# Three pairs of gate tiles computed as block products behind the branch-a outputs, with block products summed in PSUM

## The chip, the cores and the metric

The kernel runs on one core of one Trainium2 chip. The metric is the device time of one execution in microseconds (us); three runs of the kernel before gave 1294.07, 1295.1 and 1296.71, a median of 1295.1. The engines are TensorE (PE in the profile; its weight loads are PEld), VectorE (DVE), ScalarE (ACT), GpSimd (POOL) and SyncE (SP), each of which takes its instructions in the order in which they are issued.

## The reference

One step of a hybrid encoder layer on 576 rows (512 of a new stream, 64 of a running one), model width 1024. A half-step SwiGLU FFN of width 2816, a mixer with two convolution branches and gates, a second half-step FFN, a final RMSNorm. What matters here is the mixer:

```python
p = h @ w_in
a_b, a_c, a_v, b_u, gate_a, gate_b = jnp.split(p, cuts, axis=-1)
a_conv, new_a = causal_depthwise_conv(a_c * a_v, hist_a, conv_a_w)
y_a = (a_b * a_conv) @ w_a_out
glu = b_u[..., :D_B] * jax.nn.sigmoid(b_u[..., D_B:])
b_conv, new_b = causal_depthwise_conv(glu, hist_b, conv_b_w)
b_act = jax.nn.silu(layer_norm(b_conv + conv_b_bias, conv_b_ln_g, conv_b_ln_b))
y_b = b_act @ w_b_out
merged = jax.nn.sigmoid(gate_a) * y_a + jax.nn.sigmoid(gate_b) * y_b
x = x + merged @ w_out
```

`gate_a` is called p5 below, `gate_b` p6; each has eight output tiles of 128 columns.

## The kernel before

Activations lie transposed, 128 channels by T = 576 rows per tile, in two halves of H = 288. Every operand of a product is split into a high part and a low part (`high`, `low`), and a tile product is the sum of three: high by high, high by low, low by high. An output tile of a 1024-deep product is 8 deep tiles x 3 x 2 halves = 48 matmuls of 128x128 by 128x288; two of them, a "plain pair", are 96. Most of the FFN's gate and up tiles, and two pairs of the branch-b outputs, are computed as "block pairs" instead: of two output tiles and two halves, seven products of 12 matmuls each (`block`, L452; 84 in all) are taken, on sums and differences of weight tiles (made by `Stream.add`, planned in `plan_block`, L350) and of input halves (`Forms`, L643), and put together from the seven by half-size sums.

In the block pairs of before each of the seven products gets a PSUM bank of its own. ScalarE copies the first bank out (288 columns), and seven half-size sums on VectorE make the two output tiles (`steps` in `pair`, L863, and in `block_pair`, L1240). PSUM is a pool `mm` of four tiles of two banks.

All engine calls go through `Ordered` (L88 in the profile for every instruction), which keeps each engine's instructions in the order of the code. Work that can float is kept in the list `work`; `fill` takes a piece from it whenever an estimate of VectorE's time lags behind an estimate of TensorE's. What has to be done with a finished product is run one product later, by `take`. Weights come through `Stream`: SyncE loads a raw tile, ScalarE casts it to the high part, and the low part is made either by GpSimd's accumulating DMA (`"dma"`; ScalarE then writes the negated high part first) or by VectorE (`"dve"`), some units ahead of their use.

The stage of the change begins when branch a's convolution is done. The loop at L1171 to L1178 alternates p5_j and ya_j, eight of each: `ga_of` has ScalarE take the sigmoid of p5_j out of PSUM, `ya_of` has VectorE multiply ya_j, still in PSUM, by it into `M[j]` (the buffers of x). Beside these products the LayerNorm of branch b goes on, driven by `advance` (L1149): when all eight convolution tiles `C[j]` are there, `lnsum.gather` and a total by a product with ones give the mean; `center` (L1112) subtracts it from a tile on VectorE, has ScalarE square the tile and VectorE add the square; `var.gather` splits the sum into a high part (ScalarE) and a low part (VectorE), a second total by ones gives the variance and `rstd` the factor RL. Then come the eight p6 tiles (`gb_of`, sigmoids on ScalarE) with `swish` of branch b as floating work, the branch-b outputs yb (pairs 0 and 2 plain, 1 and 3 as blocks), and the o product.

The seven products of a pair in before:

```python
for n, xs in enumerate(bs):
    q.append(block(ws.get(plan[f, "s", i][n]), xs))
    if n > 0:
        steps[n - 1]()
```

## Time and profile before

| what | us |
|---|---|
| median of 3 runs | 1295.1 |
| span of the profiled execution | 1290.1 |
| TensorE busy | 1279.4 (99%), 9728 matmuls |
| VectorE busy | 925.1 (72%) |
| ScalarE busy | 765.5 (59%) |
| GpSimd busy | 361.6 (28%) |
| p5 and ya products in the span | 645.0 to 746.2 |
| totals by ones in that stretch | 688.67 (mean), 714.48 (variance) |
| p6 products | 746.2 to 796.1 |
| branch-b outputs | 796.1 to 843.3 |
| second FFN begins | about 901 |

The profile is that of one execution; the time of a run lies about 5 us over the span. In a row of a timeline the first two numbers are start and length in us; the end of a matmul is modelled, so rows of TensorE overlap by a little, and the pace is read from start to start. In brackets stands the idle time ahead of a row and what ended it. A row of groups ends in the count, the busy time, the mean of one in ns and the idle time ahead. A row of stretches has the busy time of PE, PEld, DVE, ACT and POOL, then the granted TensorE clock, the share of DMA and GB/s.

### The profile page before, as it was taken

The page shows a single profiled execution, that of the slowest core. Times are in us where ns is not written, and L with a number is a line of the kernel's source. Part 1 is how long each engine was busy: PE and PEld are TensorE (multiplying, and loading weights), DVE is VectorE, ACT ScalarE, POOL GpSimd, SP SyncE. Part 2 cuts the span into 40 slices and gives each one's busy share as a digit, 9 for nine tenths or more (in the row PEclk, how much of TensorE's full clock was granted, in tenths as well). Part 3 has the DMA queues.
Part 4 walks back from the last instruction along what each step waited for, and adds up shares of the span by engine and source line. Part 5 has one row for each costly group of instructions (what it writes and reads, how often), then busy time and mean ns, then how long its engine had stood idle before and what let it go on. Part 6 is the DMA issues. An engine that isn't in the chain of part 4 may idle for free.

```text
span 1290.1 us, 25702 instructions
## 1 busy us (share of the span) xinstructions
PE 1279.4 (99%) x9728; PEld 1277.5 (99%) x9728; DVE 925.1 (72%) x1539; ACT 765.5 (59%) x1359; POOL 361.6 (28%) x460
## 2 busy tenths in 40 slices
PE   9999999999999999999999999999999999999997
PEld 9999999999999999999999999999999999999997
DVE  6868668748846998888895166656867848847956
ACT  7655646646776645555444576477665655654664
POOL 0032332232333444333321221122142141241230
PEclk9999999999999999999999999999999999999998
DMA  7286787886799898788885767696687696796783
GB/s 220 70 181 154 163 180 155 177 181 149 154 224 232 174 200 173 165 172 174 172 172 124 163 142 154 151 236 145 139 175 171 151 197 151 164 204 138 158 172 97
DMA packets 286812, 215.26 MB, mean 167 GB/s; under 512 B 15456, under 2 KB 248928, under 8 KB 286688
## 3 DMA queue, kind: packets, MB, share of 16 engines
q0 software_dynamic: 56160, 92.43, 43.3%
q1 hardware_dynamic: 228784, 120.35, 32.8%
q8 instruction: 77, 1.26, 0.4%
q10 hardware_dynamic: 1744, 0.83, 0.2%
q14 instruction: 47, 0.39, 0.1%
HBM read 116.17 MB, written 4.98 MB: 94 GB/s over the span
## 4 chain that ended last, share of the span: by engine, by line
PE 92%; issue 4%; DVE 2%; DMA 1%; ACT 1%; POOL 0%; DVEq 0%; POOLq 0%; ACTq 0%
PE mm L88 92%; DVE tmp L88 0%; DMA g<-raw 0%; DMA raw<-in_w_b_out_dram 0%; DVE x L88 0%; DVE g L88 0%; DMA u<-raw 0%; ACT act L88 0%; DVE w L88 0%; POOL u L88 0%; DVE act L88 0%; ACT u L88 0%; ACT w L88 0%; ACT g L88 0%; POOL g L88 0%
## 5 line engine op out<-in xcount | busy, mean ns | idle before, releaser
L88 PE MATMUL mm<-act,u 128*128 128x288 f32 x4758 | 668.3, 293 | 0.1
L88 PEld LDWEIGHTS mm<-act,u 128*128 128x128 f32 x4758 | 638.9, 188 | 0.4 <-DMA u<-raw 0.3
L88 PE MATMUL mm<-act,g 128*128 128x288 f32 x3030 | 432.9, 294 | 0.9 <-DMA g<-raw 0.9
L88 PEld LDWEIGHTS mm<-act,g 128*128 128x128 f32 x3030 | 410.3, 188 | 1.1 <-DMA g<-raw 1.1
L88 POOL DMA_DIRECT2D u<-raw x197 | 172.3, 874 | 481.7 <-ACT u L88 317.4
L88 PE MATMUL mm<-act,act 128*128 128x288 f32 (+2 forms) x1896 | 259.9, 293 | 0.0
L88 PEld LDWEIGHTS mm<-act,act 128*128 128x128 f32 x1896 | 252.2, 188 | 0.5 <-ACT act L88 0.3
L88 ACT CAST u<-raw 128x512 fp32r<-128x512 f32 (+2 forms) x207 | 118.8, 574 | 172.0 <-PE mm L88 136.7
L88 POOL DMA_DIRECT2D g<-raw x126 | 109.9, 872 | 297.4 <-ACT g L88 242.7
L88 DVE SCALAR_TENSOR_TENSOR w<-g,prm,w 128x606 f32<-128x606 f32 x232 | 179.3, 844 | 1.4 <-ACT w L88 1.4
L88 DVE TENSOR_TENSOR tmp<-mm,tmp 128x288 f32<-128x288 f32 (+1 forms) x251 | 112.9, 459 | 70.3 <-PE mm L88 53.7
L88 ACT ACTIVATE u<-u 128x512 fp32r<-128x512 f32 (+2 forms) x197 | 116.8, 593 | 6.2
L88 ACT CAST g<-raw 128x512 fp32r<-128x512 f32 (+2 forms) x136 | 75.1, 553 | 43.9 <-DMA raw<-in_ffn_w_down_dram 17.6
L88 DVE SCALAR_TENSOR_TENSOR tmp<-mm,r 128x576 f32<-128x576 f32 x48 | 36.3, 757 | 76.6 <-PE mm L88 76.6
L88 POOL DMA_DIRECT2D act<-raw x67 | 59.1, 883 | 108.3 <-ACT act L88 94.5
L88 ACT CAST act<-tmp 128x576 fp32r<-128x576 f32 x92 | 61.9, 675 | 43.1 <-DVE tmp L88 42.1
L88 ACT CAST g<-w 128x512 fp32r<-128x512 f32 x79 | 49.0, 620 | 64.4 <-DVE w L88 58.6
L88 ACT CAST u<-w 128x512 fp32r<-128x512 f32 x81 | 50.2, 619 | 61.0 <-DVE w L88 43.6
L88 DVE TENSOR_TENSOR act<-tmp,act 128x576 fp32r<-128x576 f32 x92 | 67.5, 754 | 18.1 <-ACT act L88 16.5
L88 ACT ACTIVATE g<-g 128x512 fp32r<-128x512 f32 (+2 forms) x126 | 72.1, 572 | 4.0
L88 DVE TENSOR_TENSOR w<-raw,raw 128x512 f32<-128x512 f32 x82 | 56.2, 685 | 16.2 <-DMA raw<-in_ffn_w_gate_up_dram 11.2
L88 ACT ACTIVATE tmp<-tmp 128x576 f32<-128x576 f32 x47 | 32.2, 686 | 45.1 <-DVE tmp L88 45.0
(86 smaller groups left out, 830.6 us busy)
## 6 DMA issues: line engine op xcount, KB each, us to landing
raw<-in_ffn_w_gate_up_dram SPq DMA_DIRECT2D x171, 256.0 KB, 3.5
u<-raw POOLq DMA_DIRECT2D x140, 256.0 KB, 4.2
raw<-in_w_in_dram SPq DMA_DIRECT2D x112, 256.0 KB, 3.8
raw<-in_ffn_w_down_dram SPq DMA_DIRECT2D x96, 192.0 KB, 3.8
g<-raw POOLq DMA_DIRECT2D x69, 256.0 KB, 4.2
act<-raw POOLq DMA_DIRECT2D x61, 256.0 KB, 4.4
g<-raw POOLq DMA_DIRECT2D x43, 192.0 KB, 4.5
u<-raw POOLq DMA_DIRECT2D x41, 192.0 KB, 4.5
```

The source lines that it names most:

```text
L88: return self.tc.keep_in_program_order(fn(*args, **kwargs))
```

## The change

Three things change. First, every block pair (39 in the FFNs, two in yb) now goes through one function, `seven`. The order of the second and third product is swapped; products five and six aren't given banks of their own but are summed into the banks of products one and two. ScalarE copies both banks out after product two (576 columns, one instruction), and one finished bank after product six (288 columns); VectorE makes five half-size sums, not seven.

Second, the eight p5 tiles no longer alternate with ya. The order is p5_0, ya_0 to ya_7, p5_1, p6_0, then three block pairs for p5_2 to p5_7, then p6_1 to p6_7. As ya_j now comes ahead of its gate, ScalarE copies it to `M[j]` (for j of 1 to 7), and VectorE multiplies by the gate later (`gated`). The input forms for the blocks are made by VectorE, as sums of the high and low parts that are there, with differences of halves (`whole`) and a split in high and low (`part`).

Third, the mean's total comes between ya_7 and p5_1, and the centring, squares and the variance's total run beside the three block pairs, one step of `between` after each of the 21 products.

```diff
-                (s2, "dve", ((s2, (s1, a11)),)),
-                (s1, "dve", ()),
+                (s1, "dve", ((s2, (s1, a11)),)),
+                (s2, "dve", ()),
...
+    def seven(ws7, xs7, c1, c2, gate, between=None):
+        qq, uu = ttile(), ttile()
+        u2, u3 = half(uu, 0), half(uu, 1)
+        first, second = psum2(), psum2()
+        q = [first[:, 0, :H], first[:, 1, :H], second[:, 0, :H], second[:, 1, :H]]
+        def middle():
+            dve.tensor_tensor(u2, q[2], half(qq, 0), op=ALU.subtract)
+            dve.tensor_tensor(u3, q[3], u2, op=ALU.add)
+            dve.tensor_tensor(half(c2, 1), u3, half(qq, 1), op=ALU.subtract)
+        def close():
+            sca.copy(half(c1, 0), q[0])
+            dve.tensor_tensor(half(c1, 1), q[1], u2, op=ALU.subtract)
+            gate()
+        steps = {
+            1: lambda: sca.copy(halves(qq), first[:, :, :H]),
+            3: middle,
+            5: close,
+        }
+        last = bank()[:, :H]
+        for n, (w, xs) in enumerate(zip(ws7, xs7)):
+            block(ws.get(w), xs, (q + q[:2] + [last])[n], n not in (4, 5))
+            if n in steps:
+                steps[n]()
+            if between:
+                between()
+        return lambda: dve.tensor_tensor(half(c2, 0), last, u3, op=ALU.add)
...
+        def first():
+            sca.activation(c1, c1, AF.Sigmoid)
+            gated(j, c1)
+        def second():
+            final()
+            sca.activation(c2, c2, AF.Sigmoid)
+        def between():
+            take()
+            if later:
+                later.pop(0)()
+            advance()
+            fill()
+        final = seven(plan["p5", "s", i], bs, c1, c2, first, between)
+        later.extend((second, lambda: gated(j + 1, c2)))
```

ScalarE's queue before, from the sigmoid of p5_5 (`tmp_1351`) to that of p5_6 (`tmp_1363`); the rest makes weight parts:

```order
L88 ACTIVATE tmp_1351_9127<-mm_1336_8991 128x576
L88 CAST act_1353_9130<-raw_1332_8933 128x512
L88 ACTIVATE act_1354_9131<-act_1353_9130 128x512
L88 CAST u_1356_9161<-raw_1334_8963 128x512
L88 ACTIVATE u_1356_9161<-u_1356_9161 128x512
L88 CAST u_1359_9193<-raw_1339_8997 128x512
L88 ACTIVATE u_1359_9193<-u_1359_9193 128x512
L88 CAST u_1361_9223<-raw_1341_9027 128x512
L88 ACTIVATE u_1361_9223<-u_1361_9223 128x512
L88 ACTIVATE tmp_1363_9253<-mm_1352_9129 128x576
```

And now, from the close of pair one to the copy of pair two's first two banks (`tmp_1337` is c1 of pair one and `tmp_1338` its c2, `g_969` a tile of the LayerNorm, `mm_1373` the two first banks of pair two):

```order
L88 COPY tmp_1337_9040<-mm_1341_9044 128x288
L88 ACTIVATE tmp_1337_9040<-tmp_1337_9040 128x576
L88 CAST act_1366_9183<-w_1364_9161 128x512
L88 ACTIVATE tmp_1368_9199<-g_969_5725 128x576
L88 CAST u_1376_9211<-raw_1288_8753 128x512
L88 ACTIVATE u_1376_9211<-u_1376_9211 128x512
L88 ACTIVATE tmp_1338_9041<-tmp_1338_9041 128x576
L88 CAST act_1381_9237<-raw_1360_9125 128x512
L88 ACTIVATE act_1382_9238<-act_1381_9237 128x512
L88 COPY tmp_1371_9204<-mm_1373_9206 128x576
```

The sigmoids of pair one, a square of the LayerNorm and four weight instructions stand between the close of pair one and that copy. VectorE's queue, at the last centrings before (`g_1033` and `g_1047` are tiles of the LayerNorm, `tmp_1304` the mean, `x4` a gated output):

```order
L88 TENSOR_TENSOR g_1033_6212<-g_1033_6212,tmp_1304_8758 128x576
L88 TENSOR_TENSOR acc_1306_8765<-acc_1306_8765,tmp_1325_8916 128x576
L88 TENSOR_TENSOR g_1047_6359<-g_1047_6359,tmp_1304_8758 128x576
L88 TENSOR_TENSOR acc_1306_8765<-acc_1306_8765,tmp_1326_8920 128x576
L88 TENSOR_TENSOR tmp_1328_8923<-acc_1306_8765,tmp_1327_8922 128x576
L88 TENSOR_TENSOR x4_94<-mm_1329_8927,tmp_1335_8989 128x576
```

And now, from the middle of pair one to the sum that makes its last half, the one that writes `tmp_1338` from `mm_1343`:

```order
L88 TENSOR_TENSOR tmp_1338_9041<-tmp_1340_9043,tmp_1339_9042 128x288
L88 TENSOR_TENSOR u_1361_9127<-w_1353_9080,u_1361_9127 128x512
L88 TENSOR_TENSOR act_1363_9146<-w_1359_9123,act_1362_9145 128x512
L88 TENSOR_TENSOR w_1364_9161<-w_1353_9080,raw_1347_9055 128x512
L88 TENSOR_TENSOR tmp_1337_9040<-mm_1341_9044,tmp_1340_9043 128x288
L88 TENSOR_TENSOR x2_92<-x2_92,tmp_1337_9040 128x576
L88 TENSOR_TENSOR g_969_5725<-g_969_5725,mu_1351_9075 128x576
L88 TENSOR_TENSOR acc_1352_9077<-acc_1352_9077,tmp_1368_9199 128x576
L88 TENSOR_TENSOR act_1367_9184<-w_1364_9161,act_1366_9183 128x512
L88 TENSOR_TENSOR w_1375_9209<-raw_1348_9057,raw_1349_9059 128x512
L88 TENSOR_TENSOR tmp_1338_9041<-mm_1343_9046,tmp_1340_9043 128x288
```

The centrings now stand among the weight sums and the half-size sums of the pairs. TensorE's queue at the variance's total, before, between two plain products:

```order
L88 MATMUL mm_1344_9056<-tmp_1327_8922,ones_r_83 128x288
L88 MATMUL mm_1344_9056<-tmp_1328_8923,ones_r_83 128x288
L88 MATMUL mm_1344_9056<-tmp_1327_8922,ones_r_83 128x288
L88 MATMUL mm_1344_9056<-tmp_1328_8923,ones_r_83 128x288
L88 MATMUL mm_1345_9065<-act_1085_6735,act_1319_8849 128x288
```

And now, between the sixth product of pair three (`mm_1399`) and its seventh (`mm_1401`):

```order
L88 MATMUL mm_1399_9358<-act_952_5574,u_1394_9340 128x288
L88 MATMUL mm_1424_9501<-tmp_1415_9453,ones_r_83 128x288
L88 MATMUL mm_1424_9501<-tmp_1416_9454,ones_r_83 128x288
L88 MATMUL mm_1424_9501<-tmp_1415_9453,ones_r_83 128x288
L88 MATMUL mm_1424_9501<-tmp_1416_9454,ones_r_83 128x288
L88 MATMUL mm_1401_9360<-act_1329_9024,act_1402_9362 128x288
```

The total moved from between two plain products to the inside of a block pair.

More of the change, by code (lines that the diff above doesn't have):

```diff
@@ L365, in plan_block @@
         ]
-        ws.second.update(plan[name][n] for n in (1, 5, 6))
+        ws.second.update(plan[name][n] for n in (2, 5, 6))
     def plan_ffn(f, gu, dn):
@@ L450, in chunks, with block @@
         return got
-    def block(w, xs):
-        q = bank()[:, :H]
+    def block(w, xs, q, new):
         for k in range(KU):
@@ L1143, in then, with gb_of @@
         def then(ps):
-            dve.tensor_tensor(halves(M[j]), ps, halves(gates.pop(j)), op=ALU.mult)
-        return then
-    stage, held = [0], [0]
+            if j in gates:
+                dve.tensor_tensor(halves(M[j]), ps, halves(gates.pop(j)), op=ALU.mult)
+            else:
+                sca.copy(halves(M[j]), ps)
+        return then
+    def gb_of(j):
+        def then(ps):
+            while work and j >= 2 and len(BA) < j - 1:
+                work.pop(0)()
+            sg = wtile(n=T) if j < 2 else gtile(n=T)
+            sca.activation(halves(sg), ps, AF.Sigmoid)
+            SGB.append(sg)
+        return then
+    stage, held = [1], [0]
     def advance():
         nonlocal var, mu, RL
-        if stage[0] == 0 and len(C) == KT and not work:
-            lnsum.gather()
-        elif stage[0] == 1:
-            mu = ttile()
-            sca.mul(halves(mu), lnsum.total(), 1.0 / D)
+        if stage[0] == 1:
+            mu = rpool.tile([P, T], F32, tag="r", name=nm("mu"), bufs=2)
+            sca.mul(halves(mu), sums, 1.0 / D)
             var = Sum()
@@ L1192, in tile_encoder_step @@
     ws.ahead = 4
-    def gb_of(j):
-        def then(ps):
-            while work and j >= 2 and len(BA) < j - 1:
-                work.pop(0)()
-            sg = wtile(n=T) if j < 2 else gtile(n=T)
-            sca.activation(halves(sg), ps, AF.Sigmoid)
-            SGB.append(sg)
-        return then
-    for j in range(KT):
+    for j in range(1, KT):
         product(("p", 6, j), xg, gb_of(j))
@@ L1241, in block_pair, with between @@
         j = 2 * i
[L1242 to L1251 removed]
+        c1, c2 = ttile(), ttile()
         def first():
[L1254 removed]
             dve.tensor_tensor(c1, c1, SGB[j], op=ALU.mult)
             merged(j, c1)
[L1258 to L1270 removed]
+        def between():
+            if i == KU - 1 and between.n == 4:
+                MS[4], MS[5] = split(M[4]), split(M[5])
+            between.n += 1
+        between.n = 0
+        seven(plan["yb", "s", i], bs, c1, c2, first, between)()
         dve.tensor_tensor(c2, c2, SGB[j + 1], op=ALU.mult)
```

121 lines of the change are left out of this document (68 added, 53 removed).

## The prediction

> **What bounds the kernel now.** I read the page first: its span, its first and its fourth part.
>
> ```profile
> span 1290.1 us, 25702 instructions
> PE 1279.4 (99%) x9728; PEld 1277.5 (99%) x9728; DVE 925.1 (72%) x1539; ACT 765.5 (59%) x1359; POOL 361.6 (28%) x460
> ...
> PE 92%; issue 4%; DVE 2%; DMA 1%; ACT 1%; POOL 0%; DVEq 0%; POOLq 0%; ACTq 0%
> ```
>
> PE works for 1279.4 of 1290.1 us and carries 92% of the chain that ended last. So a change pays by what PE does less, and costs by every time PE is made to wait. The profiled span is 1290.1 us; the median of the three runs is 1295.1, which is 5.0 us over it. I sum against the span and add these 5.0 at the end. Next come PE's timeline in the stage that is changed, and in the branch-b outputs, which hold block pairs today.
>
> ```profile
> 689.20 3.32 PE L88 MATMUL mm<-act,act 128*128 128x288 f32 x24
> ...
> 714.48 0.69 PE L88 MATMUL mm<-tmp,ones_r 128*128 128x288 f32 x4
> ...
> 743.09 12.64 PE L88 MATMUL mm<-act,u 128*128 128x288 f32 x96
> 755.57 3.28 PE L88 MATMUL mm<-act,act 128*128 128x288 f32 x24
> ```
>
> ```profile
> 808.61 1.74 PE L88 MATMUL mm<-act,u 128*128 128x288 f32 x12
> ...
> 819.70 3.33 PE L88 MATMUL mm<-act,u 128*128 128x288 f32 x24
> ...
> 845.70 4.50 PE L88 MATMUL mm<-act,g 128*128 128x288 f32 x32 [0.86 <-DMA g<-raw]
> ```
>
> A plain pair of output tiles is 96 matmuls: from 743.09 to 755.57, 12.48 us (130.0 ns each). A block pair is 84: from 808.61 to 819.70, 11.09 us, so one of its seven products takes 1.584. Between the two totals by ones the plain pace is a little lower: 689.20 to 714.48 is 25.28 us for 192 matmuls, 131.7 ns each. In the whole stretch nothing waits; the one stall nearby is 0.86 us at 845.70, on a weight tile that came late.
>
> The last question is what else runs where the new pairs go. The view of stretches answers for the end of the gate tiles, VectorE's timeline for the centring of the LayerNorm.
>
> ```profile
> 715.00:752.40 37.40, 37.40 (x290) 37.40 (x289) 4.81 (x7) 16.57 (x26) 10.34 (x12) 1.00 0.80 170
> ```
>
> ```profile
> 696.29 0.76 DVE L88 TENSOR_TENSOR acc<-acc,tmp 128x576 f32<-128x576 f32 x1 [0.75 <-ACT tmp L88]
> 696.97 0.75 DVE L88 TENSOR_TENSOR g<-g,tmp 128x576 f32<-128x576 f32 x1
> 698.47 0.76 DVE L88 TENSOR_TENSOR acc<-acc,tmp 128x576 f32<-128x576 f32 x1 [0.75 <-ACT tmp L88]
> ```
>
> VectorE (third engine column) works 4.81 of the last 37.4 us of the gate stage: there is room. But centring is a ping-pong. VectorE subtracts the mean at 696.97, ScalarE squares, and VectorE can add the square only at 698.47: 1.50 us from the one to the other, 0.75 of it waiting. Before, nothing that PE needs stood behind that wait. Now something does.
>
> **The change part by part.** The prices of single instructions:
>
> ```profile
> L88 DVE TENSOR_TENSOR tmp<-mm,tmp 128x288 f32<-128x288 f32 x246 | 109.2, 453 | 70.1 <-PE mm L88 53.7 <-ACT tmp L88 9.1 <-ACT g L88 3.2
> L88 DVE TENSOR_TENSOR act<-tmp,act 128x576 fp32r<-128x576 f32 x92 | 67.5, 754 | 18.1 <-ACT act L88 16.5
> L88 DVE TENSOR_TENSOR w<-raw,raw 128x512 f32<-128x512 f32 x82 | 56.2, 685 | 16.2 <-DMA raw<-in_ffn_w_gate_up_dram 11.2 <-DMA raw<-in_w_b_out_dram 5.0
> ```
>
> ```profile
> L88 ACT CAST act<-raw 128x512 fp32r<-128x512 f32 x65 | 39.7, 611 | 6.4 <-PE mm L88 3.0 <-DMA raw<-in_ffn_w_gate_up_dram 2.1 <-DMA raw<-in_w_in_dram 1.2
> L88 ACT ACTIVATE act<-act 128x512 fp32r<-128x512 f32 x61 | 38.6, 634 | 1.9
> L88 ACT ACTIVATE tmp<-tmp 128x576 f32<-128x576 f32 x47 | 32.2, 686 | 45.1 <-DVE tmp L88 45.0
> ...
> L88 ACT COPY tmp<-mm 128x288 f32<-128x288 f32 x41 | 15.8, 384 | 9.0 <-PE mm L88 9.0
> ...
> L88 ACT COPY tmp<-mm 128x576 f32<-128x576 f32 x8 | 5.0, 623 | 0.0
> ```
>
> Back to back an instruction starts about 0.08 us before the one ahead has ended (0.76 at 696.29, the next 0.68 later), so I step VectorE by 0.68 for 576 columns, 0.61 for 512, 0.45 for a half that needs the one ahead and 0.38 for one that doesn't; ScalarE by 0.6.
>
> *PE's work.* Three pairs lose 12 matmuls each: 3 x (12.48 - 11.09) = -4.2 us. At the lower plain pace a pair is 12.64 and the three bring -4.6; I take -4.2.
>
> *New work on VectorE in the stage.* The input forms are made before the pairs start: per pair of inputs two sums of high and low part and four half-size differences, then two low parts, some 4 x (2 x 0.68 + 4 x 0.45 + 2 x 0.68) = 18 us. They begin some 25 us ahead of the first pair, beside plain products, beside which VectorE had 4.81 us in 37.4 to do. I cost them at nothing, with those products of PE as cover; a form that came late would hold PE by as much as it is late. Inside the pairs VectorE has, for three pairs, 15 half-size sums, the weight sums and low parts of 21 tiles, seven centrings of two instructions and the gating products: about 33 us of work in 3 x 11.09 = 33.3 us of PE. It has no slack, and it works in order with ScalarE.
>
> *The new wait.* Products five and six of a pair are summed into the banks of products one and two. So product five can't start before ScalarE has copied both banks out. Product five starts 4 x 1.584 = 6.34 us after its pair. Everything in ScalarE's queue ahead of that copy now holds PE. I follow the chain through pair two, in us from the start of pair one, with PE unhindered so far:
>
> ScalarE's sigmoid of the first g_b tile waits for its product and ends at 0.65, the mean follows at 1.25. VectorE centres the first tile at 1.3. ScalarE squares it, makes one weight tile (1.2), copies pair one's banks (4.5) and squares the second tile, so VectorE adds it at 5.2, centres the third at 5.9, adds it at 7.4, makes two weight tiles (9.3), the three middle sums of pair one (10.5), three weight tiles (12.4), the half that closes tile c1 (12.8); it waits 0.75 for the sigmoid, gates at 13.6, centres (14.25), adds 1.50 later at 15.75, makes two weight tiles and comes to the last half of pair one at 17.65. The sigmoid of that tile stands ahead of pair two's copy on ScalarE and starts at 18.1; a cast and the product behind it take 1.2, the copy 0.6: done at 20.6. PE wants product five of pair two at 11.09 + 6.34 = 17.4. **PE waits 3.2 us.**
>
> Pair three, counted from 17.65: up to the last half of pair two VectorE has five halves (2.2), six instructions of 576 (4.1) and seven of 512 (4.3), 10.6 together, and waits for two squares, two sigmoids and ScalarE's queue (about 3.3): it gets there 13.9 later. Then a half (0.45), the sigmoid, one square, two weight instructions and the copy on ScalarE (five steps of 0.6 to 0.65): 17.4. PE, set back to 20.6, wants product five of pair three 11.09 after that, so 14.0 after 17.65. **PE waits another 3.4.** The total by ones of the variance is put ahead of the last product, two products (3.2) on, at 20.6; the last two squares and sums, then the high and the low part of the sum (0.68 and 0.76), end at 21.6: **1.0 more.** Together +7.6. Bounds: if each step ran 10% shorter the second and third pair would wait 2.0 and 1.8 and the total 0.5 less, 4.3; if ScalarE's queue held two more weight steps in each, 1.2 more each, 10.0.
>
> *The same rule in the other block pairs.* They use it too: ScalarE now copies 576 columns (623 against 384 ns, 0.24 more), and product five must wait for it. In most pairs there is room, as in this one:
>
> ```profile
> 1011.16 0.38 ACT L88 COPY tmp<-mm 128x288 f32<-128x288 f32 x1
> 1013.04 1.74 PE L88 MATMUL mm<-act,g 128*128 128x288 f32 x12
> ```
>
> The copy would end at 1011.78, product five starts at 1013.04: 1.26 us to spare. In the first pair of each FFN ScalarE is late:
>
> ```profile
> 914.49 1.74 PE L88 MATMUL mm<-act,g 128*128 128x288 f32 x12
> ...
> 915.19 0.38 ACT L88 COPY tmp<-mm 128x288 f32<-128x288 f32 x1
> ```
>
> ```profile
> 63.17 1.74 PE L88 MATMUL mm<-act,g 128*128 128x288 f32 x12
> 63.41 0.39 ACT L88 COPY tmp<-mm 128x288 f32<-128x288 f32 x1
> ```
>
> In the second FFN it would end at 915.81, 1.3 after product five was to start; in the first at 64.04, 0.9 after. That is +2.2, between 0 (if the copy gets ahead of the casts) and 2.7 (with the next pair late too). VectorE's five sums instead of seven in a pair save nothing, since PE waits for none of them.
>
> *The stall at 845.70.* The weight tiles ahead change places in their pools, so this DMA may land in another buffer: between -0.9 and 0; for want of a row I take the middle, -0.5.
>
> **Sum:** -4.2 + 7.6 + 2.2 - 0.5 = +5.1 us: a span of 1295.2 and, with the 5.0 around it, **1300.2 us**. With all bounds at their low ends (-4.2 + 4.3 + 0 - 0.9) it would be 1294.3, with all at their high ends (-4.2 + 10.0 + 2.7 + 0) 1303.6.
>
> **The rivals.**
>
> *VectorE keeps up (faster).* If the copy of pairs two and three is done before product five, none of the 7.6 is paid. The point is a chain 3.2 us shorter than mine over 17: a fifth. For it: VectorE's busy sum just fits. Against: the 0.75 us waits of the centring are in the trace and can't be overlapped by an engine that works in order. Time: 1290.1 - 4.2 + 2.2 - 0.5 + 5.0 = 1292.6.
>
> *It catches up once (no change).* After PE has slid by 3.2 us, pair three may find VectorE ahead: then 3.2 alone remains, 1295.8. Against: the chain of pair three is longer than PE's pair by itself.
>
> *The clock falls in the waits (slower still).* The end of the trace, by stretches, then by PE's last instructions:
>
> ```profile
> 1283.00:1283.50 0.50, 0.00 (x0) 0.00 (x0) 0.47 (x2) 0.00 (x0) 0.00 (x0) 0.72 0.57 190
> 1283.50:1284.00 0.50, 0.00 (x0) 0.00 (x0) 0.47 (x2) 0.00 (x0) 0.00 (x0) 0.50 0.00 0
> ```
>
> ```profile
> 1281.21 0.73 PE L88 MATMUL mm<-tmp,ones_r 128*128 128x272 f32 x2 [0.54 <-ACT tmp L88]
> ```
>
> PE ended at 1281.94. The granted clock (last column but two) is 0.72 on average between 1283.0 and 1283.5 and 0.50 behind, so it fell at about 1283.2: 1.3 us of rest after a sparse stretch were enough. Two waits of over 3 us could do the same, while 0.86 at 845.70 lies in a stretch without a fall. At half the clock one product of 1.584 costs 1.6 more. After the first wait the loss would vanish in the second, since the copy sets its end; after the last it stays, so +1 to +3: 1301 to 1303. [...]
>
> **How the numbers follow.** My forecast 0.64; it catches up once 0.12; the clock falls 0.14; VectorE keeps up 0.10. About 0.2% (2.6 us) is what a measurement can tell from no change, so "same" is 1292.5 to 1297.7. Of my own 0.64, 0.05 lies under 1297.7. Slower: 0.59 + 0.14 = 0.73; same: 0.05 + 0.10 = 0.15; faster: 0.10 + 0.02 = 0.12, the 0.02 from the second rival. The range leaves out the case of VectorE keeping up and the tail above: 1293.5 to 1304.
>
> **What would show it.** Right: PE idle of about 3 us, released by ScalarE's copy, before product five of pairs two and three, and about 1 us before the ones; 0.9 and 1.3 us in the FFNs' first pairs; a stage of three pairs of 41 us in place of 37.4. Wrong: pairs of 11.1 us without a gap, a wait for an input form or a weight tile in place of the copy, or a gap in most FFN pairs (then I misread the 1.26 us of room).

## The result, and the profile after

The changed kernel takes 1312.81 us in the median of five runs (1310.1 to 1317.07), the kernel before 1294.65 (five runs, 1291.55 to 1296.71): a ratio of 1.0147, 95% interval 1.0122 to 1.0171. It is slower by about 18 us, on the side that was forecast, but three and a half times as much (18.2 for 5.1) and outside the range. The page of the changed kernel, its first and fourth part:

```profile
span 1311.0 us, 25559 instructions
PE 1282.8 (98%) x9692; PEld 1278.1 (97%) x9692; DVE 935.4 (71%) x1528; ACT 800.8 (61%) x1427; POOL 357.7 (27%) x457
...
PE 77%; DVE 8%; issue 8%; ACT 4%; DMA 2%; POOL 0%; DVEq 0%; POOLq 0%; ACTq 0%
```

The 36 matmuls are gone, and the span is 20.9 us longer. PE carries 77% of the chain instead of 92%; VectorE, ScalarE, DMA and issue have taken the rest. The view of waits says whom PE waits for (us in total, times, longest):

```profile
PE mm L88 <- ACT tmp L88: 10.8, 9, 3.7
PE mm L88 <- DMA u<-raw: 5.0, 3, 3.4
PE mm L88 <- DMA g<-raw: 3.2, 3, 1.4
```

Nineteen us in 15 waits; before it was 1.4: 0.9 for a weight tile, and 0.5 for ScalarE at the end of the kernel, which every run has. (A wait of 1.0 for GpSimd at the start is in both and is left out.) Three kinds are new: eight waits for ScalarE's copies out of PSUM, one weight tile that is 3.4 us late, and five others 0.7 to 1.4 us late. PE's timeline from the first gate pair on:

```profile
720.27 1.74 PE L88 MATMUL mm<-act,act 128*128 128x288 f32 x12
...
731.36 1.75 PE L88 MATMUL mm<-act,u 128*128 128x288 f32 x12
...
741.53 1.84 PE L88 MATMUL mm<-act,u 128*128 128x288 f32 x12 [3.67 <-ACT tmp L88]
...
755.89 2.52 PE L88 MATMUL mm<-act,act 128*128 128x288 f32 x12 [3.01 <-ACT tmp L88]
758.22 2.66 PE L88 MATMUL mm<-act,u 128*128 128x288 f32 x12
760.71 0.69 PE L88 MATMUL mm<-tmp,ones_r 128*128 128x288 f32 x4
...
785.60 2.91 PE L88 MATMUL mm<-act,u 128*128 128x288 f32 x20 [3.38 <-DMA u<-raw]
```

Pair one takes 11.09 us (720.27 to 731.36). Product five of pair two waits 3.67, that of pair three 3.01. Behind the second wait two products take 2.33 and 2.49 us (start to start) in place of 1.58. The total by ones doesn't wait. At 785.60, among the plain p6 products, comes a wait that the forecast didn't have. ScalarE's queue ahead of the copy of pair two is the one that the order shows:

```profile
739.10 0.68 ACT L88 ACTIVATE tmp<-tmp 128x576 f32<-128x576 f32 x1 [1.22 <-DVE tmp L88]
739.69 0.60 ACT L88 CAST act<-raw 128x512 fp32r<-128x512 f32 x1
740.32 0.63 ACT L88 ACTIVATE act<-act 128x512 fp32r<-128x512 f32 x1
740.86 0.62 ACT L88 COPY tmp<-mm 128x576 f32<-128x576 f32 x1
```

The sigmoid waits for VectorE's last half of pair one, two weight steps follow, and the copy ends at 741.48; PE starts at 741.53. The clock behind the second wait, by stretches (last column but two):

```profile
755.80:757.00 1.20, 1.10 (x7) 1.11 (x8) 1.17 (x3) 1.17 (x4) 0.67 (x1) 0.92 0.46 85
757.00:758.20 1.20, 1.20 (x6) 1.20 (x6) 1.16 (x3) 1.17 (x4) 0.86 (x1) 0.50 1.13 181
758.20:759.50 1.30, 1.30 (x7) 1.30 (x7) 0.32 (x2) 1.30 (x3) 0.43 (x1) 0.50 0.91 208
759.50:760.70 1.20, 1.20 (x8) 1.20 (x8) 0.62 (x1) 0.98 (x2) 0.43 (x1) 0.70 1.19 226
```

A mean of 0.92 over 1.2 us is 0.19 us at half clock at its end, one of 0.70 is 0.72 us at its start: half clock from 756.8 to 760.2, 3.4 us.

The sum against the two spans: -4.2 for the pairs; +6.7 for the two waits; +1.7 for the clock; +3.4 in the p6 stage; in the FFNs +1.7 at product five of the two first pairs (0.37 and 1.33) and +5.9 in eight other waits. That is +15.2 of 20.9. Of the 5.7 that are left, 3.7 are the pace of plain matmuls in the mixer, which belongs to the execution and not to the change (next section); about 2 weren't broken down.

### The profile page after: what moved, and what is told of

It reads as the page before. It is cut to its first block, busy times and chain, and to the rows that moved or that the text cites. A ratio compares the mean times of both kernels' runs of the same rounds, so it can differ in the third digit from the quotient of the medians.

```text
span 1311.0 us, 25559 instructions
## 1 busy us (share of the span) xinstructions
PE 1282.8 (98%) x9692; PEld 1278.1 (97%) x9692; DVE 935.4 (71%) x1528; ACT 800.8 (61%) x1427; POOL 357.7 (27%) x457
## 4 chain that ended last, share of the span: by engine, by line
PE 77%; DVE 8%; issue 8%; ACT 4%; DMA 2%; POOL 0%; DVEq 0%; POOLq 0%; ACTq 0%
PE mm L88 77%; DVE tmp L88 3%; DVE act L88 2%; DVE w L88 1%; DMA g<-raw 1%; ACT tmp L88 1%; DMA u<-raw 1%; DVE g L88 1%; DVE u L88 1%; ACT act L88 1%; ACT u L88 1%; ACT g L88 1%; ACT w L88 0%; POOL u L88 0%; DVE x L88 0%
## 5 line engine op out<-in xcount | busy, mean ns | idle before, releaser
L88 DVE TENSOR_TENSOR tmp<-mm,tmp 128x288 f32<-128x288 f32 (+1 forms) x181 | 83.4, 461 | 31.3 <-ACT tmp L88 20.8
L88 DVE TENSOR_TENSOR act<-tmp,act 128x576 fp32r<-128x576 f32 x96 | 70.5, 754 | 41.9 <-ACT act L88 41.5
L88 ACT CAST u<-w 128x512 fp32r<-128x512 f32 x86 | 52.9, 616 | 51.8 <-DVE w L88 40.7
L88 ACT ACTIVATE tmp<-tmp 128x576 f32<-128x576 f32 x53 | 36.3, 685 | 76.7 <-DVE tmp L88 76.5
L88 DVE TENSOR_TENSOR w<-raw,raw 128x512 f32<-128x512 f32 x88 | 60.3, 685 | 29.6 <-DMA raw<-in_ffn_w_gate_up_dram 14.1
L88 DVE TENSOR_TENSOR g<-w,g 128x512 fp32r<-128x512 f32 x81 | 55.5, 686 | 26.1 <-ACT g L88 24.6
L88 DVE TENSOR_TENSOR u<-w,u 128x512 fp32r<-128x512 f32 x86 | 58.9, 685 | 20.2 <-ACT u L88 18.9
```

The costliest lines, as they stand in the source:

```text
L88: return self.tc.keep_in_program_order(fn(*args, **kwargs))
```

## The experiments

The theory after the result was the prediction's: PE is held because the banks of products one and two are taken again before ScalarE has copied them out. The rival: VectorE and ScalarE, which hand work to and fro and each work in order, have no slack in the stage, so that something PE needs comes late under any scheme.

**What repeats.** The changed kernel was profiled once more.

> The changed kernel once more, for a second profile. If the waits are the order's doing, they come back at the same places within 0.3 us (3.7 and 3.0 at product five, 3.4 in the p6 stage, 7.6 in the FFNs). If the pace of plain matmuls (131.7 ns in the mixer, 130.0 in the kernel before) belongs to the execution and not to the kernel, it may differ here; if it belongs to the kernel, it is 131.7 again.

It took 1311.65 us, span 1309.9. PE in the gate pairs, and a stretch of the mixer in the first and in the second execution of the same kernel:

```profile
739.18 3.25 PE L88 MATMUL mm<-act,u 128*128 128x288 f32 x12 [3.76 <-ACT tmp L88]
742.22 3.08 PE L88 MATMUL mm<-act,act 128*128 128x288 f32 x12
745.10 1.83 PE L88 MATMUL mm<-act,u 128*128 128x288 f32 x12
...
753.55 1.85 PE L88 MATMUL mm<-act,act 128*128 128x288 f32 x12 [0.27 <-ACT tmp L88]
```

```profile
571.38 3.32 PE L88 MATMUL mm<-act,u 128*128 128x288 f32 x24
574.54 3.32 PE L88 MATMUL mm<-act,act 128*128 128x288 f32 x24
```

```profile
567.44 3.28 PE L88 MATMUL mm<-act,act 128*128 128x288 f32 x24
570.56 3.28 PE L88 MATMUL mm<-act,u 128*128 128x288 f32 x24
```

The first wait came back at 3.76, but this time the clock fell behind it (0.50 granted from 739.0 to 745.0; 3.04 and 2.88 us for two products, 2.8 lost), and so pair three waited 0.27 and not 3.01. What the slower PE loses after the first wait it doesn't wait for at the second: the copy's end is set by the other engines. Product five of pair three starts 35.6 us behind the first pair's start in both executions (753.55 - 717.90 and 755.89 - 720.27). Not everything came back within 0.3 us: the late tile of the p6 stage did (3.18), this time with a fall of the clock behind it (20 matmuls in 4.28 us, 1.7 lost), but the ten waits in the FFNs that made 7.6 us came to 9.2, and the one of 0.85 us behind the yb products was gone. The pace of the mixer was 3.12 us per 24 matmuls here and 3.16 there. For the 2208 matmuls of the mixer that is 3.7 us, in one and the same kernel. The kernel before had 3.12 in its profile. So 3.7 of the 20.9 us are the execution's and not the change's.

**The two parts alone.** ffn_only is the kernel before with the function `seven` in the FFNs and the yb pairs; gates_only the changed kernel with the old scheme in those.

```diff
 # ffn_only: before with
+        final = seven(plan[f, "s", i], bs, t, cu, gate, between)
 # gates_only: after with
-        final = seven(plan[f, "s", i], bs, t, cu, gate, between)
+            for n, xs in enumerate(bs):
+                q.append(own_block(ws.get(plan[f, "s", i][n]), xs))
```

> The kernel before with the new function for the block pairs of the two FFNs and of the branch-b outputs; the gate stage as before. Theory (ScalarE's queue): the copy of two banks and the extra copy make ScalarE late in the FFNs, so the short waits that the changed kernel shows there (0.37, 0.52, 0.37, 0.66, 1.33, 0.75, 1.39, 0.62, 0.36, 1.19: 7.6 us, less 1.2 that before has too) all come back: 1299 to 1303 against 1294.65, and no wait at the gate tiles. Rival (they are echoes of the later gate stage, or of a slower pace of TensorE): only the two first pairs wait, 1294 to 1297.

> The changed kernel with the old scheme (seven banks) in the FFNs and the branch-b outputs; only the three pairs of gate tiles use the new one. Theory: -4.2 for 36 matmuls, +6.7 for the two waits at product five, +1.7 for the clock's fall behind the second, +3.4 for the weight tile that is late in the p6 stage: +7.6, 1300 to 1304. Rival (the waits of the gate pairs follow from the work that the FFNs' scheme leaves behind): the gate pairs run without waits and the time is 1291 to 1295.

ffn_only: 1303.34, ratio 1.0078 (1.0051 to 1.0106). gates_only: 1302.69, ratio 1.0078 (1.0054 to 1.0101). By these medians each half of the change costs about 10 us by itself. The profiles don't bear out all of it for the FFNs. In ffn_only PE waits 3.6 us for ScalarE in six waits (the view's 4.1 in seven hold the 0.5 at the end) and 2.3 for weight tiles in four; none of it is an echo of the gate stage. That is 5.0 us more than before, while the profiled span is 13.5 longer (1303.6). The pace is in it: 24 matmuls of the mixer took 3.16 us in this execution, 3.7 us over the mixer, and the 40 us of plain products ahead of it ran at 134.4 ns a matmul (18 in 2.42) instead of 131.7, 0.8 us more; the rest wasn't broken down. gates_only, whose mixer ran at 3.12 as in the kernel before, has a span 8.3 us longer and no wait over 0.2 us in the FFNs: 5.2 us for ScalarE at the gate pairs, 0.4 for VectorE at the total and 3.4 for the tile in the p6 stage, with a fall of the clock behind the first and the last of these (1.7 and 2.7 us lost).

**Is it the reuse of the banks in the gate pairs?** own_banks gives the seven products of a gate pair their own banks, but makes the middle sums at once as in the change (four of them, as it has seven sums in all); p5_old uses the whole old scheme there, each sum one product later, on gates_only.

```diff
 # own_banks, in the gate pairs
-            block(ws.get(w), xs, (q + q[:2] + [last])[n], n not in (4, 5))
+            q.append(bank()[:, :H])
+            block(ws.get(w), xs, q[n], True)
 # p5_old, in the gate pairs
+            q.append(own_block(ws.get(w), xs))
+            if n > 0:
+                steps[n - 1]()
```

> The changed kernel with seven banks and seven half-size sums in the three gate pairs, so that no product waits for a copy; the rest unchanged. Theory A (the reuse of the banks is what makes PE wait): the waits of 3.67 and 3.01 go, the clock doesn't fall, PE waits at most 1 to 3 us in another place (a late weight tile or the total by ones): 1303 to 1309 against 1312.8. Theory B (VectorE and ScalarE can't keep up in this stage, whoever asks): the waits only move, to the first product of pair three and to the total by ones, and the sum of them stays 6 to 8: 1311 to 1315.

> The run gates_only with the old scheme in the three gate pairs too: seven banks, seven half-size sums, each step one product later as in the kernel before; so the kernel before but for the order of the stage and its three block pairs. Theory A (summing into the first banks is what makes PE wait for the copy): no wait at product five, at most 1 to 2 us at a weight tile or at the total, and the late weight tile of the p6 stage stays (3.6 and perhaps the clock's 2.6): 1295 to 1299. Theory B (VectorE and ScalarE are full here): waits of 4 us or more stay, in other places of the pairs: 1300 to 1305.

own_banks: 1313.52, ratio 1.0168 (1.0140 to 1.0196), as slow as the change:

```profile
742.20 3.22 PE L88 MATMUL mm<-act,u 128*128 128x288 f32 x12 [7.74 <-DVE tmp L88]
```

PE waits 7.7 us for VectorE before product five of pair two, whose bank lies in one PSUM tile with product four's (`bank` hands out the halves of a tile in turn). The sum that reads product four ends at 742.05, and PE starts at 742.20: it waits for that reading, so the run has a shared tile in place of a shared bank and settles less than it was meant to. p5_old: 1304.5, ratio 1.0100 (1.0077 to 1.0123), no better than gates_only. It reuses no bank early and shares nothing, and PE waits 2.9 us for weight tiles in the pairs and 3.1 at the total. It has two sums more on VectorE in each pair, so it isn't the reuse alone that differs. But the theory that the banks alone hold PE falls for the gate pairs: without their early reuse the wait moves to the next thing that VectorE or ScalarE makes, as the rival has it.

**Order or amount of work?** no_centre leaves six centrings out; copy_first sets ScalarE's copy of the first two banks ahead of the last half, sigmoid and gating of the pair before; no_pingpong keeps the work and takes VectorE's direct waits apart. The last two stand on gates_only.

```diff
 # no_centre
+        if 0 < j < KT - 1:
+            var.n += 1
+            return
 # copy_first
+            count[0] += 1
+            if count[0] == 1:
+                advance()
+                return
             if later:
                 later.pop(0)()
 # no_pingpong
         dve.tensor_tensor(C[j], C[j], mu, op=ALU.subtract)
-        var.square(C[j])
         var.add(dve)
+        var.square(C[j])
...
-            gated(j, c1)
+            soon.append(lambda: gated(j, c1))
```

> The changed kernel without centring, squares and sums of six of the eight tiles of the LayerNorm (they stay out of the output): VectorE has 6 x 2.18 = 13 us less to do beside the gate pairs. Theory (the ping-pong of the centring sets ScalarE's copy back): the copy of pair two is done 3 to 5 us earlier and both waits go: 7 to 12 us under the changed kernel, 1301 to 1306, with the late weight tile of the p6 stage smaller or gone. Rival (the weight sums of the pairs alone keep VectorE too busy): waits of 2 to 3 us stay at both places and the time is 1308 to 1313.

> The run gates_only with one change in the three gate pairs: the last half of the pair before, its sigmoid and gating are issued one product later, behind the copy of the first two banks, so the copy no longer stands behind that sigmoid in ScalarE's queue. Theory (the order of ScalarE's queue makes PE wait): the copy of pair two is done about 3 us earlier; the waits at product five, 3.9 and 2.3 us with the total, fall to at most 1 together, and the clock's fall of 1.5 us behind them goes: 1294 to 1298 against 1302.7. Rival (VectorE's total work in the stage sets the pace): the waits move to the total by ones or to pair three's first product and the time stays at 1300 to 1304.

> The run gates_only with VectorE's direct waits for ScalarE taken apart in the three gate pairs: a square is added behind the next centring instead of its own, and the gating product of the first tile comes one product after its sigmoid. The work is the same. Theory (VectorE's instructions just fit the pairs, 33 of 33.3 us, and the 0.75 us waits of its in-order queue are what's too much): the waits of the stage, 6.2 us with the total and 1.5 of the clock, fall to 2 or less, and the p6 wait of 3.6 + 2.6 shrinks with them: 1294 to 1299 against 1302.7. Rival (the work itself is too much): the sum of the waits up to the variance's total stays above 5, 1300 to 1304.

no_centre went the wrong way: 1317.29, ratio 1.0197 (1.0172 to 1.0222). The wait of pair three is gone, that of pair two is still 3.2, since `rstd` with its two loads of the function table (1.28 us each) now stands ahead of that copy. And in the p6 stage PE waits 6.2 and 2.9 us in place of 3.4: the planner, which counts less work on VectorE, can issue the swish sooner, though that this is the cause wasn't shown. It says nothing clean on the centring. copy_first: 1299.88, ratio 1.0064 (1.0042 to 1.0086). Pair two's wait fell from 3.8 to 1.1, but pair three waits 2.7 and the total 2.2 and 0.2: 6.2 in place of 5.7. The time isn't told apart from gates_only's (1.0054 to 1.0101), though the p6 wait is shorter (1.8); the rival was right for the pairs. no_pingpong: 1294.41, ratio 1.0011 (0.9998 to 1.0023), 8 us under gates_only (1.0078), each set against the kernel before of its own batch. The view of waits of gates_only, then of no_pingpong:

```profile
PE mm L88 <- ACT tmp L88: 5.8, 3, 3.8
PE mm L88 <- DMA u<-raw: 3.4, 1, 3.4
```

```profile
PE mm L88 <- ACT tmp L88: 3.7, 4, 1.5
PE mm L88 <- DMA u<-raw: 1.8, 1, 1.8
```

The same instructions in another order wait 3.5 us in the pairs and at the total (0.4 for VectorE beside the first row, and without the 0.5 at the end) and not 5.7; the p6 wait is 1.8 and not 3.4; and the clock falls only behind the latter. VectorE's own waits, from the first pair's start to the end of the total, show where it comes from, again gates_only first:

```profile
DVE acc L88 <- ACT tmp L88: 6.1, 6, 1.8
```

```profile
DVE acc L88 <- ACT tmp L88: 1.3, 2, 1.1
```

In gates_only VectorE works 30.9 of these 40.4 us and waits 8.8 for ScalarE, 6.1 of them to add the squares. In no_pingpong it works 29.9 of 35.2 us and waits 5.1. So most of it isn't the amount of work but the time that VectorE stands at the squares and sigmoids, 0.75 us or more at a time, in a stage that has no slack; 3.5 us of PE's waits stayed.

**The late tile of the p6 stage.** lag is gates_only with one line behind the pairs:

```diff
     ws.ahead = 4
+    dve.time = max(dve.time, pe.time) + 4500
```

> The run gates_only with one change behind the gate pairs: the planner's count of VectorE's time is set 4.5 us ahead of TensorE's, so that the pieces of the swish are issued later among the p6 products and the casts of weight tiles stand ahead of them in ScalarE's queue. Theory (weight casts are late because they stand behind swish steps that wait for the variance): the wait of 3.6 us at the second p6 product and the fall of the clock behind it (2.6 us) go: 1295 to 1299 against 1302.7; the waits at the gate pairs stay. Rival (VectorE is late for good, and whatever it delays must show): a wait of the same size before the branch-b outputs, 1301 to 1305.

1297.0, ratio 1.0036 (1.0020 to 1.0053); 5.7 us under gates_only. The wait is gone, and nothing has come for it up to the end of the yb products (0.2 us for a weight tile behind them). In the changed kernel the cast of that tile is here:

```profile
779.33 1.41 ACT L88 CAST act<-tmp 128x576 fp32r<-128x576 f32 x2 [0.85 <-DVE tmp L88]
780.65 0.62 ACT L88 CAST u<-raw 128x512 fp32r<-128x512 f32 x1
```

ScalarE reaches it at 780.65, behind the high parts of swish tiles that waited for VectorE; GpSimd's DMA makes the low part behind it (issued at 782.22, landed 3.3 us later), and PE goes on at 785.60. The planner's count of VectorE's time holds neither VectorE's waits for ScalarE nor PE's waits, so it takes VectorE to be ready for the swish too soon; by how much wasn't measured, but 4.5 us on that count were enough.

**The FFNs.** ffn_unshared is ffn_only with own banks for products five and six; ffn_spread has VectorE's sums behind products four, five and seven; ffn_dve_copy has the second copy on VectorE; act_load is the kernel before with nothing but two more copies on ScalarE per pair.

```diff
 # ffn_unshared
-            block(ws.get(w), xs, (q + q[:2] + [last])[n], n not in (4, 5))
+            block(ws.get(w), xs, (q + [third[:, 0, :H], third[:, 1, :H], last])[n], True)
 # ffn_spread
-            3: middle,
-            5: close,
+            3: part,
+            4: middle,
+            6: close,
 # ffn_dve_copy
-            sca.copy(half(c1, 0), q[0])
+            dve.tensor_copy(half(c1, 0), q[0])
 # act_load, in the FFN pairs of before
+                sca.copy(u4, q[0])
...
+                sca.copy(half(t, 1), q[4])
```

> The run ffn_only with banks of their own for products five and six and seven half-size sums, but the same order, the same copy of two banks and the same grouping of VectorE's sums. Theory A (the reuse of the banks couples PE to ScalarE): the ten short waits in the FFNs go, 4 to 7 us under ffn_only (1303.3): 1296 to 1299. Theory B (the grouped sums make the hidden tiles and the weight parts late, whoever waits): waits of 0.5 to 1.4 us stay before the down products, 1300 to 1304.

> The run ffn_only with VectorE's five half-size sums spread over three products (one, two and one with the copy behind products four, five and seven) and the gate one product later, where the kernel before has it; the same copy and the same reuse of banks. Theory (grouping the sums and setting the gate ahead lengthens the loop from a pair's close by VectorE and ScalarE to the next pair's copy): the waits of 0.5 to 1.4 us at product five and before the down products fall from 7.2 to 3 or less: 1296 to 1300 against 1303.3. Rival (the copy of 576 columns and the second copy on ScalarE do it): 1301 to 1305.

> The run ffn_only with the copy of the finished first bank made by VectorE and not by ScalarE: 0.38 us per pair less on ScalarE, as much more on VectorE, nothing else. Theory A (ScalarE's load): the waits fall by a third to a half, 1297 to 1301 against 1303. Theory B (the grouped close on VectorE delays the silu, and all casts stand behind it): the close gets longer, so the waits grow, 1303 to 1308.

> The kernel before, its own scheme and order untouched, with two copies of 288 columns more on ScalarE in each FFN pair (0.77 us; their results are overwritten): one behind the copy of the first bank, one behind product six. No product waits for them. Theory A (the new scheme costs the FFNs time by ScalarE's extra copying, since its queue has next to no slack ahead of the down products): PE waits for weight tiles before the down products, 3 to 6 us together, 1297 to 1300 against 1293.9. Theory B (the reuse of banks and the order of VectorE's sums cost it): less than 1 us of waits, within 1.5 us of the kernel before.

ffn_unshared: 1326.98, ratio 1.0276 (1.0246 to 1.0306), far worse than ffn_only, where 4 to 7 us less was expected if the reuse of the banks costs. PE doesn't wait for a copy in the FFNs at all (its one wait for ScalarE is the 0.5 at the end), but 23.5 us for weight tiles:

```profile
PE mm L88 <- DMA g<-raw: 11.8, 9, 2.1
PE mm L88 <- DMA u<-raw: 11.7, 9, 2.3
```

So the copies' wait can be taken away, and something dearer takes its place. It has seven sums on VectorE, three of them in the close that the silu waits for. ffn_spread: 1300.13, ratio 1.0061 (1.0041 to 1.0081), against 1.0078 for ffn_only: not told apart. Its waits for copies fell from 3.6 to 2.0 us (without the 0.5 at the end), those for weight tiles rose from 2.3 to 4.5. ffn_dve_copy: 1306.11, ratio 1.0095 (1.0073 to 1.0118): also not told apart from ffn_only by its time, but the waits for copies rose from 3.6 to 6.1, so by its waits a longer queue on VectorE is worse than one on ScalarE. act_load: 1300.51, ratio 1.0050 (1.0031 to 1.0070). Nobody waits for its copies, and still weight tiles come late, five of seven times before the down products:

```profile
PE mm L88 <- DMA g<-raw: 2.4, 4, 1.3
PE mm L88 <- DMA u<-raw: 1.6, 3, 0.6
```

4.0 us of waits. Two causes then. ScalarE's extra work makes the tiles behind a group late, which act_load shows alone (with 0.77 us in each pair, where the new function adds 0.62). The waits at product five come from a loop, which the copies of the second FFN's last group show in the changed kernel, with PE's row at the end:

```profile
1196.76 0.64 ACT L88 COPY tmp<-mm 128x576 f32<-128x576 f32 x1 [1.87 <-PE mm L88]
1208.31 0.62 ACT L88 COPY tmp<-mm 128x576 f32<-128x576 f32 x1
1220.26 0.62 ACT L88 COPY tmp<-mm 128x576 f32<-128x576 f32 x1
1232.19 0.62 ACT L88 COPY tmp<-mm 128x576 f32<-128x576 f32 x1
1244.13 0.62 ACT L88 COPY tmp<-mm 128x576 f32<-128x576 f32 x1
```

```profile
1193.41 1.74 PE L88 MATMUL mm<-act,g 128*128 128x288 f32 x12
...
1204.45 1.74 PE L88 MATMUL mm<-act,u 128*128 128x288 f32 x12
...
1244.80 1.85 PE L88 MATMUL mm<-act,g 128*128 128x288 f32 x12 [0.62 <-ACT tmp L88]
```

PE's pairs start 11.04 us apart (1193.41, 1204.45), the copies 11.55, then 11.95, 11.93, 11.94. From close to gate, silu, casts and copy, and by the copy to the next close, the other engines need 0.9 us more than PE per pair. The first pair of a group has 2.3 us to spare (the copy ends at 1197.40, product five starts at 1199.72); in the fifth they are used up. The copies of the other runs tell what sets the loop's length. Two in a row of the same group, in ffn_spread and in ffn_unshared:

```profile
1220.59 0.62 ACT L88 COPY tmp<-mm 128x576 f32<-128x576 f32 x1
1232.13 0.62 ACT L88 COPY tmp<-mm 128x576 f32<-128x576 f32 x1
```

```profile
1231.44 0.62 ACT L88 COPY tmp<-mm 128x576 f32<-128x576 f32 x1
1244.19 0.62 ACT L88 COPY tmp<-mm 128x576 f32<-128x576 f32 x1
```

The step is 11.94 us in ffn_only as in the change, 11.54 in ffn_spread, where the sums are spread and the gate comes later, 12.25 in ffn_dve_copy with a copy on VectorE in place of ScalarE, and 12.75 in ffn_unshared with two sums more on VectorE. So the loop's length follows VectorE's sums and their place. ffn_spread has no wait at product five in the last group of either FFN, where ffn_only has four (0.4 to 0.6). In ffn_unshared no copy holds PE back, and a loop 1.7 us longer than PE's pair fits its late tiles. What keeps ffn_spread 0.5 us over 11.04 stays open.

**Together.** loose has no_pingpong, copy_first, lag, an earlier mean and the variance's total behind p6_1; pingpong_lag only the two that paid; pingpong_lag_mean also the earlier mean. All have the old scheme in the FFNs.

```diff
 # pingpong_lag_mean, ahead of the pairs
     bs = xforms.operands(xg, False)
+    advance()
 # loose, besides
+            if stage[0] < 3:
+                advance()
...
+    product(("p", 6, 1), xg, gb_of(1))
```

> All that the runs so far point to, on the old scheme in the FFNs: no_pingpong, the copy ahead of the last half (copy_first), the mean made before the first pair, the variance's total behind the first plain p6 product, and the planner's shift (lag). Theory: waits of at most 1.5 us in the gate pairs, none at the total or in the p6 stage, so the 36 matmuls saved show: 3 to 5 us under the kernel before (1291.0), 1285.5 to 1289. Rival (the variance now comes 6 us later and the swish must end before the branch-b outputs): waits of 3 us or more before those, 1290 to 1295.

> The two changes that paid, together: the gate pairs with the old scheme in the FFNs, VectorE's direct waits taken apart (no_pingpong, 1294.4) and the planner's shift behind the pairs (lag, which took 3.6 and 2.6 us of the p6 stage away). no_pingpong still had 1.9 and 1.7 there. Theory: these go, 4.3 us of waits in the pairs stay against 4.7 saved: 1289.5 to 1292 against 1293.9. Rival (waits in one queue only move): a wait of 2 to 4 us shows before the branch-b outputs and the time stays at 1293 to 1296.

> pingpong_lag with the mean made by ScalarE ahead of the last input forms and the sigmoid of the first p6 tile, so that VectorE can centre from the first pair's start on, about 1 us earlier. Theory: the waits at product five of pairs two and three and at the total, 4.3 us, fall by 1 to 2: 1288 to 1291. Rival (ScalarE's queue, not VectorE's start, sets the copies): no difference from pingpong_lag beyond 1 us.

loose: 1295.8, ratio 1.0019 (1.0007 to 1.0031), not the gain that was expected: nothing waits at the total or among the p6 products, but pairs two and three wait 1.4 and 2.7 us, the clock fell behind the second (the next product took 3.05 us in place of 1.58), and two weight tiles come 0.5 and 0.7 late from the yb products on. pingpong_lag: 1292.97, ratio 0.9986 (0.9973 to 0.9999). pingpong_lag_mean: 1290.91, ratio 0.9984 (0.9973 to 0.9996); the same waits (3.7 us for ScalarE, 0.4 for VectorE), so the earlier mean did nothing that shows, as its rival said. Both are a little faster than the kernel before. The runs of each lie in two groups (last section), and group against group the gain stays: for pingpong_lag 1289.5 to 1290.9 and 1293.0 to 1293.7, for the kernel before 1289.7 to 1292.2 and 1294.1 to 1296.8. The gate pairs can pay, but with 3.5 us of waits left 0.1 to 0.2% is all that the 36 matmuls bring.

## Why the prediction was wrong

**Right: the pairs' pace and the chain through pair two.** Pair one took 11.09 us as taken from the yb pairs. The copy of pair two was put at 20.6 us after the first pair's start; it ended at 21.2 (741.48 - 720.27), and the wait was 3.67 for 3.2. Pair three: 3.01 for 3.4. The input forms, put at nothing, held nothing: PE has no wait between 360.88 and 741.53.

**Right as a rival: the clock.** It fell behind the second wait in one execution (1.7 us) and behind the first in the other (2.8). In the second the next wait shrank to 0.27, as the text had worked out. The total by ones, which was to wait 1.0 us, waited 0 in the first: VectorE's low part ended at 760.13 and PE came at 760.71, which at full clock would have been 759.06. Pairs, clock and total come to 8.3 us for 7.6; that this is so near is partly luck, as the sum held no clock, and without it the stage came to 6.7. What length of rest brings the fall the runs don't show: in the first execution one came behind 3.01 us and none behind 3.67, in the second one behind 3.76, and in no_pingpong one behind 1.75 (last section). Half clock lasted 3.4 us behind the 3.01 and behind the 1.75; behind the 3.76 the granted clock was 0.50 in all four stretches from 739.0 to 745.0.

**Wrong: "In most pairs there is room".** This step carried the largest error: the term of 2.2 us came to 7.6, of which 5.9 lie outside the two first pairs. It read the spare time (1.26 us) off one pair of the kernel before and moved the copy by 0.24. But where the copy stands isn't fixed by PE: it is the end of a loop through VectorE and ScalarE, which the change makes longer than PE's pair. Lateness adds up at 0.9 us per pair and shows four pairs later. And tiles behind the group were no term at all, though ScalarE got 0.62 us more to do in each pair; in act_load 0.77 us more in each pair alone made 4.0 us of such waits. The first pairs themselves came to 0.4 and 1.3 for 0.9 and 1.3.

**Wrong: what is late next.** The sum ended with the pairs. It asked what PE waits for there, and not what the late variance does behind them: weight casts queued behind swish steps, 3.4 us, which the sum put at nothing. In lag, where the swish steps are issued later, the wait is gone.

**Wrong: the 5.0 us around the span.** The time is 1.8 us over the span in the changed kernel (1312.81 and 1311.0). The profile of before was of an execution with the quicker pace, and its span was compared with a median that holds both. By 1.8 the forecast would have been 3.2 lower, so this error hid part of the other.

**The stall at 845.70** was to lose 0.5; it stayed at 0.85 us in its new place in the first execution and was gone in the second.

**The rivals.** VectorE didn't keep up, and didn't catch up. That its instructions and waits fill the pairs was right: from the first pair's start to the end of the total it works 30.9 us and waits 8.6 for ScalarE, of 41.0; that the waits more than the work are too much, no_pingpong showed. The bounds (4.3 to 10.0) held the stage's own sum. The range failed because it was built around one stage, when 7.6 us of waits lie in the FFNs, which the change touches 39 times, and 3.4 behind the pairs; 3.7 more were the pace of the execution.

## What to carry to other kernels

When PE is at 99%, a change that saves matmuls must be summed over every place where an engine that works in order gets a new wait ahead of something PE needs, with the loop's period and not the spare time of one turn: a loop 0.9 us longer than PE's turn showed nothing for four turns here. The accumulation that saved VectorE two sums in a pair saved nothing here, where VectorE was busy for 72% of the span: ffn_only was 0.78% slower than the kernel before. And each copy that it put on ScalarE stands ahead of weight casts: in act_load two copies more in a pair (0.77 us) came with 4.0 us of waits for weight tiles. Where two engines hand work to and fro, reorder first: adding the square and gating one step later took 8 us off in no_pingpong with the same instructions.

## What the runs showed of the hardware

The pace of plain matmuls in the mixer showed two values, 130.0 and 131.7 ns (24 in 3.12 or 3.16 us), and one kernel can have either in the same stretch in different executions, as the two profiles of the changed kernel show. The 29 runs of the kernel before lie in two groups, 12 from 1289.7 to 1292.2 and 17 from 1294.1 to 1296.8, with nothing between; those of pingpong_lag_mean in two as well, 1289.9 to 1291.1 and 1293.1 to 1294.1. Two profiled runs tie the groups to the two paces (3.7 us in the mixer): that of pingpong_lag, with 3.16 us, took 1293.74, that of pingpong_lag_mean, with 3.12 and the same waits, 1290.16. For the other runs of the groups the pace isn't known. What sets it stays open. Differences of 0.2% between two single runs of this kernel say nothing.

In no_pingpong half clock came behind a rest of 1.75 us. PE rests there once, for the late tile of the p6 stage, between plain products on both sides; the stretches behind it:

```profile
773.90:775.00 1.10, 1.10 (x8) 1.10 (x8) 1.10 (x3) 0.84 (x3) 0.00 (x0) 0.92 1.03 168
775.00:778.00 3.00, 3.00 (x14) 3.00 (x14) 2.93 (x7) 2.94 (x6) 1.25 (x2) 0.50 0.68 185
778.00:779.00 1.00, 1.00 (x9) 1.00 (x8) 1.00 (x2) 1.00 (x3) 0.47 (x1) 0.88 1.12 194
```

That is half clock from 774.8 to 778.2, again 3.4 us, and 1.7 us lost. A wait of 1.76 us at the same place in copy_first had a fall behind it too (the next 20 matmuls took 3.81 us, in the changed kernel 2.75); waits of 3.67 and 3.38 us in the changed kernel had none (granted clock 1.00 from 741.5 to 750.0 and from 785.6 to 788.0).
